# Spreading twelve small loads and re-dealing table work in the first feed-forward block of a decoder trunk

## The chip, the core and the metric

The kernel runs on one core of one Trainium2 chip. The core has five engines that run side by side and wait for one another through semaphores: TensorE (PE, with its weight loads shown apart as PEld), VectorE (DVE), ScalarE (ACT), GpSimd (POOL) and SyncE (SP), which here only issues transfers. Sixteen DMA engines move the data. Every engine takes its instructions in the order in which the program gives them. The metric is the device time of one execution in microseconds, lower is better. The kernel before took 982.28 us (median of three runs, 981.8 to 982.3).

## What is computed

The reference is a two-layer trunk on 256 rows of 1024 columns. Each layer is half a SwiGLU block, a mixer, and half a SwiGLU block; the mixer of layer 0 is a diagonal state-space layer (S5), that of layer 1 is block-sparse attention.

```python
def swiglu(h, w_gate, w_up, w_down):
    return (jax.nn.silu(h @ w_gate) * (h @ w_up)) @ w_down
...
for layer in range(DEPTH):
    h = h + MACARON_WEIGHT * swiglu(rms_norm(h, ffn_norm[layer, 0]), ffn_w_gate[layer, 0],
                                    ffn_w_up[layer, 0], ffn_w_down[layer, 0])
    hn = rms_norm(h, mix_norm[layer])
    ...
    h = h + MACARON_WEIGHT * swiglu(rms_norm(h, ffn_norm[layer, 1]), ffn_w_gate[layer, 1],
                                    ffn_w_up[layer, 1], ffn_w_down[layer, 1])
```

The S5 mixer uses, for each of 64 groups, a state of 64 complex numbers with decay `lam`, an input matrix from `b_re`, `b_im` (64 x 64 x 16 each) and an output matrix from `c_re`, `c_im` (64 x 16 x 64 each):

```python
bu_re = jnp.einsum('bcgn,gpn->bcgp', u_c, bb_re)
...
pr, pi, sr, si = lax.associative_scan(combine, (lam_re_b, lam_im_b, bu_re, bu_im), axis=1)
...
y = jnp.einsum('bcgp,gnp->bcgn', st_re, c_re) - jnp.einsum('bcgp,gnp->bcgn', st_im, c_im)
```

## The kernel before

**Stages.** The phases run one after the other: `f00` (first SwiGLU block), `s5`, `f01`, `f10`, `moba`, `f11`. What this text is about lies in `f00`, where the kernel also works out, beside the matmuls, the tables that `s5` will read.

**Weights.** Each weight is used as a sum of two parts, `whi` and `wlo`, and each product is three matmuls. `Stream` brings the weights as units of 1 MB into three buffers called `raw`, on SP's queue. A unit is then split in two halves, and a split (L86, L87) is an ACT instruction that writes `whi` and a DVE instruction that writes `wlo`. When the second half of a unit is split, its `raw` buffer is free, and the load of the unit three further on is given to SP's queue at that place of the program. SP therefore waits for DVE's `wlo` before each weight load, and everything given to SP later stands behind it. In `f00` a split is only placed once its unit's load lies AGE = 8 slots back.

**Slots.** While `f00` is written out, a counter called slot stands for the progress of TensorE: `fill` adds 0.7 for every three matmuls of 512 columns (1.4 in the first group). Everything that is placed between the matmuls is placed by this counter.

**Groups.** `f00` goes through 11 groups `j` of 256 hidden columns. `gu(j, t)` makes gate and up for half `t` of the rows (8 steps of three matmuls). `gated` then applies SiLU on ACT (L480, `sg`) and multiplies on DVE (L484, `act`). Later `tr(j, t)` transposes `act` on TensorE (L497), and ACT and DVE copy the result as `ah` and `al` (L499, L500). `dn(j, f)` multiplies it with the down weights. I write g(j,a) for the two gate/up units of group j, and d(j) for its down unit. Between `gated(j, t)` and `tr(j, t)` lie 7 slots from group 1 on: `gated(2, 0)` is placed at slot 30.8 and `tr(2, 0)` at 37.8, for instance.

**Tables.** `tables` is a generator which `fill` resumes once per step. It holds three lists. `loads` are twelve transfers, given to SP's queue when the slot reaches the number in LOADS: eight for B (`ld_b4`, 64 KB each, in runs of 16 floats) and four for C (`ld_c2`, 128 KB each, in runs of 64 floats). `work` is DVE's table work in order: the doubling steps of the powers (`e_init`, `e_step`, from slot E_AT = 26), the products of B (`b_all`), then for each of 8 blocks two `muls` and two `sums`, and `spread`. Each item has a price; a credit grows by DENSE times the slots passed, is capped at 1.5, and an item is placed when the credit covers its price. `later` holds pieces that use TensorE: four transposes of C (`c_tr`, L826, from slot C_AT = 44), and for each block a `t3_tab` (L884) and two `t1_tab` (L866), the first LAG = 12 slots after the block's `spread` and at least PACE = 4 slots apart. `spread(b)` may only be placed after three pieces of block b-2 are done, so from the third block on the pieces' pace of 12 slots per block leads. At its end `tables` gives SP the first loads of the finished tables (`TA`, `TE`, `TB`, L951 to L959).

Of the kernel before, what the change touches and what calls it, by code (L numbers as in the profile page):

```python
# [29 lines left out]
AO = (68, 68, 68, 68)  # L30
OO = 68

LOADS = (16, 16.5, 17, 17.5, 18, 18.5, 19, 19.5, 22, 24, 26, 28)
C_AT, E_AT, B_AT, DENSE, LAG, PACE, AGE = 44, 26, 36, 0.46, 12, 4.0, 8.0


class Stream:
# [83 lines left out]
def trunk_kernel(ctx: ExitStack, tc, x, ffn_norm, ffn_w_gate, ffn_w_up, ffn_w_down, mix_norm,  # L121
# [498 lines left out]
    def tables(tp):  # L620
# [26 lines left out]
        def ld_b4(i, c):  # L647
            b = (s5_b_re, s5_b_im)[i]
            nc.sync.dma_start(bn[i][:, 8 * c:8 * c + 8], bass.AP(tensor=b.tensor, offset=b.offset + 16384 * c,
                                                                 ap=[[16, 128], [2048, 8], [1, 16]]))  # L650

        def ld_c2(i, a):
            c = (s5_c_re, s5_c_im)[i]
            nc.sync.dma_start(cn[:, i, 4 * a:4 * a + 4], bass.AP(tensor=c.tensor, offset=c.offset + 32768 * a,
                                                                 ap=[[64, 128], [8192, 4], [1, 64]]))

        loads = [lambda i=i, c=c: ld_b4(i, c) for c in range(4) for i in range(2)]
        loads += [lambda i=i, a=a: ld_c2(i, a) for a in range(2) for i in range(2)]
        yield
        dtb = tp.tile([32, 2, 64], F32, name="dtb")  # L660
        nc.scalar.activation(dtb, ldt[:, :, None].to_broadcast([32, 2, 64]), AF.Exp)
# [258 lines left out]
        done = [-4]  # L920
        dma = list(zip(LOADS, loads))
        credit, then = 0.0, slot[0]
        while work or later or dma:
            now = slot[0]
            credit, then = min(credit + DENSE * (now - then), 1.5), now
            while dma and dma[0][0] <= now:
                dma.pop(0)[1]()
            if later and later[0][0] <= now:
                f = later.pop(0)
                f[1](*f[2:])  # L930
                done[0] += 1
            while work and work[0][1] <= now and credit >= work[0][0] and done[0] >= work[0][4]:
                w, _, f, pe, _ = work.pop(0)
                f[0](*f[1:])
                credit -= w
                t = max([now + LAG] + [a[0] + PACE for a in later])
                later += [(t + PACE * k,) + a for k, a in enumerate(pe)]
            yield
# [386 lines left out]


    tab = tables(tabp) if "s5" in phases else iter(())
    next(tab, None)
    slot = [0]
# [145 lines left out]
```

## Time and profile before

| | |
|---|---|
| median of three runs | 982.28 us |
| the profiled execution's own time | 982.36 us |
| its span on the core | 980.4 us |
| instructions | 17231 |
| time outside the span | 1.96 us |
| `f00`, from its second group to its last transposition | about 21 to 205 us |
| first matmul of `s5` that reads a table (L1009) | 222.5 us |

The page of the profile counts an engine as busy while an instruction of it runs, and names for idle time what ended it. The timeline lists an engine's instructions by start; a row with x2 is two instructions in a row, and a bracket at its end gives the idle time ahead and what ended it. Matmul records overlap (0.39 us long, started every 0.23 us), so a wait shorter than the overlap hides in them; the distance from start to start shows it. SPq rows are the moments at which SP issues a transfer.

### The profile page before, as it was taken

What the parts mean: (1) busy time and instruction counts of PE and PEld (TensorE: products, weight loads), DVE (VectorE), ACT (ScalarE), POOL (GpSimd) and SP (SyncE); (2) the same over time, 40 slices, a digit from 0 to 9 for tenths busy, and PEclk for the clock granted to TensorE, in tenths of its full rate; (3) what the DMA queues carried; (4) which work ended last, traced back from release to release, by engine and by line L of the source; (5) the groups of instructions that cost most, each with busy time, mean ns of one, the idle gap of its engine ahead of it and who ended that gap; (6) DMA issues with size and microseconds to landing.
All of it is one profiled execution on the core that took longest, in us unless ns stands there. A gap on an engine that the chain in (4) does not pass through costs nothing.

```text
span 980.4 us, 17231 instructions
## 1 busy us (share of the span) xinstructions
PE 972.2 (99%) x6727; PEld 867.5 (88%) x6727; DVE 688.8 (70%) x1118; ACT 560.4 (57%) x1008; POOL 186.5 (19%) x364
## 2 busy tenths in 40 slices
PE   9999999999999999999999999999999999999998
PEld 7878888788888999999999999998788899999997
DVE  5799767768768676666667766665789667766662
ACT  7565766553267555555456655544897556655540
POOL 6963544416511000000010000000441010000000
PEclk9999999999999999999999999999999999999999
DMA  8988877887645666565536656562544546656531
GB/s 284 249 269 279 275 261 242 298 324 245 252 173 182 213 208 215 172 212 175 172 125 214 221 173 214 173 215 92 172 145 157 186 143 214 231 174 213 172 130 44
DMA packets 140002, 198.74 MB, mean 203 GB/s; under 512 B 18232, under 2 KB 111504, under 8 KB 139664
## 3 DMA queue, kind: packets, MB, share of 16 engines
q1 hardware_dynamic: 133808, 184.32, 57.5%
q0 software_dynamic: 5536, 12.71, 3.6%
q8 instruction: 53, 0.87, 0.4%
q10 hardware_dynamic: 576, 0.61, 0.3%
q14 instruction: 29, 0.24, 0.1%
HBM read 183.89 MB, written 13.66 MB: 202 GB/s over the span
## 4 chain that ended last, share of the span: by engine, by line
PE 94%; DVE 2%; ACT 2%; issue 1%; POOL 1%; DMA 1%; SPq 0%; POOLq 0%; DVEq 0%; ACTq 0%
PE pM L554 13%; PE pM L553 13%; PE pM L555 13%; PE pA L399 9%; PE pA L401 9%; PE pA L400 9%; PE pM L399 6%; PE pM L400 6%; PE pM L401 6%; PE pA L473 1%; PE pR L1052 1%; PE pR L333 1%; DVE wlo L87 1%; PE pA L1090 1%; PE pR L866 1%
## 5 line engine op out<-in xcount | busy, mean ns | idle before, releaser
L553 PE MATMUL pM<-xa,whi 128*128 128x256 f32 x1056 | 295.7, 280 | 0.0
L554 PE MATMUL pM<-xa,whi 128*128 128x256 f32 x1056 | 294.9, 279 | 0.0
L555 PE MATMUL pM<-xa,wlo 128*128 128x256 f32 x1056 | 294.7, 279 | 0.0
L93 DVE SCALAR_TENSOR_TENSOR wlo<-raw,gT,whi 128x512 fp32r<-128x512 f32 x328 | 228.1, 748 | 71.2 <-ACT whi L92 71.0
L87 DVE TENSOR_TENSOR wlo<-raw,whi 128x1024 fp32r<-128x1024 f32 (+1 forms) x155 | 187.5, 1225 | 56.0 <-ACT whi L86 54.8
L92 ACT ACTIVATE whi<-raw,gT 128x512 fp32r<-128x512 f32 x328 | 213.7, 711 | 16.4 <-PE pA L401 14.6
L554 PEld LDWEIGHTS pM<-xa,whi 128*128 128x128 f32 x1056 | 198.5, 188 | 2.6
L553 PEld LDWEIGHTS pM<-xa,whi 128*128 128x128 f32 x1056 | 198.5, 188 | 2.3
L555 PEld LDWEIGHTS pM<-xa,wlo 128*128 128x128 f32 x1056 | 198.5, 188 | 0.0
L86 ACT ACTIVATE whi<-raw 128x1024 fp32r<-128x1024 f32 (+1 forms) x155 | 158.7, 1049 | 26.1 <-DMA raw<-in_ffn_w_up_dram 9.8
L399 PE MATMUL pA<-whi,ah 128*128 128x512 f32 x352 | 138.8, 394 | 0.0
L400 PE MATMUL pA<-wlo,ah 128*128 128x512 f32 x352 | 137.6, 391 | 0.0
L401 PE MATMUL pA<-whi,al 128*128 128x512 f32 x352 | 137.6, 391 | 0.0
L568 ACT ACTIVATE sg<-gr 128x256 f32<-128x256 f32 x66 | 27.6, 418 | 165.7 <-DVE gr L565 165.7
L399 PE MATMUL pM<-whi,xa 128*128 128x512 f32 (+1 forms) x304 | 122.2, 402 | 0.0
L400 PE MATMUL pM<-wlo,xa 128*128 128x512 f32 (+1 forms) x304 | 115.8, 381 | 0.1
L401 PE MATMUL pM<-whi,xa 128*128 128x512 f32 (+1 forms) x304 | 115.5, 380 | 0.0
L348 POOL TENSOR_TENSOR ms<-ss 128x1 f32<-128x1 f32 x10 | 1.9, 193 | 470.3 <-ACT sq L345 470.3
L401 PEld LDWEIGHTS pA<-whi,al 128*128 128x128 f32 x352 | 66.1, 188 | 14.3
L399 PEld LDWEIGHTS pA<-whi,ah 128*128 128x128 f32 x352 | 66.1, 188 | 11.6
L400 PEld LDWEIGHTS pA<-wlo,ah 128*128 128x128 f32 x352 | 66.2, 188 | 11.3
L565 DVE TENSOR_TENSOR gr<-pM,rrow 128x512 f32<-128x512 f32 x66 | 45.5, 689 | 40.9 <-PE pM L555 40.8
(269 smaller groups left out, 1214.5 us busy)
## 6 DMA issues: line engine op xcount, KB each, us to landing
raw<-in_ffn_w_down_dram SPq DMA_DIRECT2D x44, 1024.0 KB, 5.4
raw<-in_ffn_w_gate_dram SPq DMA_DIRECT2D x80, 512.0 KB, 4.0
raw<-in_ffn_w_up_dram SPq DMA_DIRECT2D x80, 512.0 KB, 5.1
raw<-in_moba_w_qkv_dram SPq DMA_DIRECT2D x12, 1024.0 KB, 5.1
TB<-dB SPq DMA_DIRECT2D x8, 768.0 KB, 6.6
raw<-in_ffn_w_gate_dram SPq DMA_DIRECT2D x16, 256.0 KB, 4.4
raw<-in_ffn_w_up_dram SPq DMA_DIRECT2D x16, 256.0 KB, 4.7
dB<-tt POOLq DMA_DIRECT2D x16, 256.0 KB, 5.1
```

Of the source, the lines that this page charges most:

```text
L86: nc.scalar.activation(hi[:, c], r[:, c], AF.Copy)
L87: nc.vector.tensor_tensor(lo[:, c], r[:, c], hi[:, c].bitcast(F32), op=OP.subtract)
L92: nc.scalar.activation(hi[:, c], r[:, c], AF.Identity, scale=g)
L93: nc.vector.scalar_tensor_tensor(lo[:, c], r[:, c], g, hi[:, c].bitcast(F32), op0=OP.mult, op1=OP.subtract)
L399: mm(o, xh, wh, start=start, stop=False)
L400: mm(o, xh, wl, start=False, stop=False)
L401: mm(o, xl, wh, start=False, stop=stop)
L553: mm(o, a, xh, start=k == 0 and i == 0, stop=False, skip_group_check=True)
L554: mm(o, a, xl, start=False, stop=False, skip_group_check=True)
L555: mm(o, b, xh, start=False, stop=k == 7, skip_group_check=True)
L565: V.tensor_tensor(gr, ps.rearrange("p (i c) -> p i c", i=2), Rr["row"][:, None, :].to_broadcast([128, 2, 256]), op=OP.mult)
L568: nc.scalar.activation(sg, gr[:, 0, :], AF.Silu)
```

## The change

Three things change: the twelve loads get other slots, C's four come ahead of B's eight, and DENSE becomes two numbers with a slot at which the second takes over. Every instruction of the old program is in the new one; only the order on the queues differs.

```diff
-LOADS = (16, 16.5, 17, 17.5, 18, 18.5, 19, 19.5, 22, 24, 26, 28)
-C_AT, E_AT, B_AT, DENSE, LAG, PACE, AGE = 44, 26, 36, 0.46, 12, 4.0, 8.0
+LOADS = (20, 21, 22, 23, 24, 26, 28, 30, 32, 34, 36, 38)
+C_AT, E_AT, B_AT, DENSE, LAG, PACE, AGE = 44, 26, 36, (64, 0.39, 0.51), 12, 4.0, 8.0
...
-        loads = [lambda i=i, c=c: ld_b4(i, c) for c in range(4) for i in range(2)]
-        loads += [lambda i=i, a=a: ld_c2(i, a) for a in range(2) for i in range(2)]
+        loads = [lambda i=i, a=a: ld_c2(i, a) for a in range(2) for i in range(2)]
+        loads += [lambda i=i, c=c: ld_b4(i, c) for c in range(4) for i in range(2)]
...
-            credit, then = min(credit + DENSE * (now - then), 1.5), now
+            credit, then = min(credit + DENSE[1 + (now > DENSE[0])] * (now - then), 1.5), now
```

## The prediction

> **What bounds the kernel now.** I read the page first: TensorE is busy throughout and carries the chain of waits, so a change elsewhere pays only where TensorE stands still.
>
> ```profile
> span 980.4 us, 17231 instructions
> PE 972.2 (99%) x6727; PEld 867.5 (88%) x6727; DVE 688.8 (70%) x1118; ACT 560.4 (57%) x1008; POOL 186.5 (19%) x364
> PE 94%; DVE 2%; ACT 2%; issue 1%; POOL 1%; DMA 1%; SPq 0%; POOLq 0%; DVEq 0%; ACTq 0%
> ```
>
> Next came the sums by stretch over the first block, which show where TensorE (first figure) falls short of a stretch: 0.70 us between 40 and 50, 0.19 between 50 and 60, and only 0.92 in all of 21 to 207 us. In brackets are counts; the last two figures are the DMA share and GB/s.
>
> ```profile
> 20.00:30.00 10.00, 9.97 (x47) 7.65 (x46) 7.29 (x13) 7.45 (x12) 8.55 (x19) 1.00 0.89 303
> 30.00:40.00 10.00, 10.00 (x47) 8.22 (x46) 8.15 (x12) 6.07 (x8) 9.35 (x16) 1.00 0.94 167
> 40.00:50.00 10.00, 9.30 (x44) 7.36 (x43) 7.58 (x21) 3.73 (x6) 9.21 (x25) 1.00 1.07 332
> 50.00:60.00 10.00, 9.81 (x51) 7.91 (x50) 9.96 (x16) 7.34 (x12) 9.92 (x20) 1.00 0.88 259
> ...
> 21.00:207.00 186.00, 185.08 (x980) 149.05 (x980) 145.47 (x219) 115.66 (x185) 97.52 (x169) 1.00 0.85 269
> ```
>
> TensorE's timeline names the two places. Matmuls start every 0.23 us (48.38 to 48.61); the transposition of act(2,0) starts 1.09 us after the matmul ahead of it. So 1.09 - 0.23 = **0.86 us** are lost there. The second, 0.19 us, stands before a transposition of C.
>
> ```profile
> 48.38 0.39 PE L400 MATMUL pM<-wlo,xa 128*128 128x512 f32 x1
> 48.61 0.39 PE L401 MATMUL pM<-whi,xa 128*128 128x512 f32 x1
> 49.70 0.44 PE L497 MATMUL pR<-cst,act 128*128 128x128 f32 x2 [0.70 <-DVE act L484]
> ...
> 59.66 0.63 PE L826 MATMUL pR<-cst,cn 128*64 128x128 f32 x4 [0.19 <-ACT cb L829]
> ```
>
> Then I went back from act(2,0). On DVE it ends at 49.17 + 0.47 = 49.64, behind a split that began at 45.29 after 1.71 us of idling for ACT. On ACT that split waited 6.14 us for a weight load, and `sg` for act(2,0) stood behind it.
>
> ```profile
> 43.28 0.30 DVE L628 TENSOR_TENSOR e<-z,z 128x32 f32<-128x32 f32 x2
> 45.29 1.27 DVE L87 TENSOR_TENSOR wlo<-raw,whi 128x1024 fp32r<-128x1024 f32 x1 [1.71 <-ACT whi L86]
> ...
> 49.17 0.47 DVE L484 SCALAR_TENSOR_TENSOR act<-pM,rr,sg 128x256 f32<-128x256 f32 x1
> ```
>
> ```profile
> 44.20 2.01 ACT L86 ACTIVATE whi<-raw 128x1024 fp32r<-128x1024 f32 x2 [6.14 <-DMA raw<-in_ffn_w_up_dram]
> ...
> 46.38 0.47 ACT L480 ACTIVATE sg<-pM,rr 128x256 f32<-128x256 f32 x1
> ```
>
> The late load is g(3,0), issued at 37.75 and 38.90. Its buffer came free with the second of the two splits from 31.31, at 31.31 + 2.44 = 33.75. SP wasn't waiting for it: from 31.10 on its rows follow without a gap, six loads of B, one of which held the queue 3.36 us.
>
> ```profile
> 31.31 2.44 DVE L87 TENSOR_TENSOR wlo<-raw,whi 128x1024 fp32r<-128x1024 f32 x2
> ...
> 36.85 2.39 DVE L87 TENSOR_TENSOR wlo<-raw,whi 128x1024 fp32r<-128x1024 f32 x2
> ```
>
> ```profile
> 30.69 0.37 SPq L182 DMA_DIRECT2D raw<-in_ffn_w_down_dram  x1
> 31.10 0.47 SPq L649 DMA_DIRECT2D bn<-in_s_b_re_dram  x1
> 31.62 0.58 SPq L649 DMA_DIRECT2D bn<-in_s_b_im_dram  x1
> 32.24 3.36 SPq L649 DMA_DIRECT2D bn<-in_s_b_re_dram  x1
> ...
> 37.75 1.10 SPq L176 DMA_DIRECT2D raw<-in_ffn_w_gate_dram  x1
> 38.90 0.51 SPq L176 DMA_DIRECT2D raw<-in_ffn_w_up_dram  x1
> ```
>
> So the chain is: B's burst on SP, g(3,0) 4.0 us late, ACT idle, DVE idle, act(2,0) late, 0.86 us of TensorE.
>
> **The loads.** The change puts no load between d(1), issued at 30.69, and g(3,0): C begins at slot 20.3, and g(3,0) is given to SP at 19.6. So g(3,0) is issued at 33.75, not 37.75. In this stretch a weight load took 3.9 to 8.7 us to land:
>
> ```profile
> DMA to landing us min/median/max: 3.9/5.2/8.7
> ```
>
> Its second half goes out some 0.5 us later, so it lands between 38.1 and 42.9, about 39.5 by the median. DVE is ready for its split at 43.28 + 0.30 = 43.58, and ACT's part takes 2.01/2 = 1.0 us: even the late end (43.9) costs DVE 0.3 us only. The pieces ahead of act(2,0) are the same in both programs (`e_init` and three `e_step`, slots 26.6 to 29.4). From the split's start to act's end is 49.64 - 45.29 = 4.35 us, so act(2,0) ends at 43.58 + 4.35 = 47.9, at worst 48.2. TensorE comes for it at 48.61 + 0.23 = 48.84. The wait is gone: **-0.86 us**, with 0.6 to 0.9 us to spare. What is late next is act(2,1):
>
> ```profile
> 58.15 0.47 DVE L484 SCALAR_TENSOR_TENSOR act<-pM,rr,sg 128x256 f32<-128x256 f32 x1
> ```
>
> It ended 58.62 - 49.64 = 8.98 us after act(2,0), with a DVE full from 50 to 60, and has the same pieces ahead of it in both programs. It will end at 47.9 + 9.0 = 56.9; its transposition, which stood two instructions ahead of the 59.66 row, is due about 58.2. No wait. The 0.19 at 59.66 is ACT's lateness with C's copies, of the same origin; I take it as gone: **-0.2 us** (bounds 0 and -0.3).
>
> The loads themselves cost what they did. From 20 to 30 us a busy share of 0.89 moved 3.03 MB. From 30 to 40 a share of 0.94 moved 1.67 MB, of which B is 0.5: the 1.17 MB of weights take 8.9 x 1.17/3.03 = 3.4 us, which leaves 6.0 us for B's eight loads, 0.75 us each. They now go out singly or by two or three from slot 24 to 38, each ahead of a weight load by at most 2.3 us, against a burst of 4.5; C's four stand together behind g(3,0), where SP must wait for g(3,1)'s buffer in any case (the first split from 36.85, so 36.85 + 2.39/2 = 38.0). `more_loads`, due at slot 30, comes among B's, long before its first use at slot 50. The needs are far off: C at slot 44, B at 53.2, the last load at 38.5. I cost the rest of the loads at nothing; the cover is that a split is placed 8 slots (8.8 us at the 1.1 worked out below) after its load, against 5.2 to land. If a B load in front uses up that cover, the same kind of wait comes back: +0.9 at most for one.
>
> [...]
>
> **The table work.** The replay of the credit rule gives the slots. With 0.39, DVE's pieces fall behind: the first `spread` comes at 70.7, not 65.8. From there the pace of the TensorE pieces (12 slots a block) leads in both programs, so 0.51 buys little: all `t3_tab` and `t1_tab` come 4.9 slots later and the generator ends at 175.7, not 170.8, still before the last transposition at 176.4. DVE's bunch of a block (one `muls`, two `sums`) stands nearest ahead of an act at 0.7 slots in both: before at 88.9 for the act at 89.6, after at 105.7 for the one at 106.4. The tightest act of before beyond 60 us is the one behind that bunch:
>
> ```profile
> 111.27 0.47 DVE L484 SCALAR_TENSOR_TENSOR act<-pM,rr,sg 128x256 f32<-128x256 f32 x1
> ```
>
> ```profile
> 113.86 0.38 PE L497 MATMUL pR<-cst,act 128*128 128x128 f32 x2
> ```
>
> ```profile
> 85.15 1.22 DVE L628 TENSOR_TENSOR z<-cb,l 128x1024 f32<-128x1024 f32 x1
> 86.40 0.69 DVE L628 TENSOR_TENSOR zc<-z,z 128x512 f32<-128x512 f32 x1
> ```
>
> It was ready 113.86 - 111.74 = 2.1 us early. Before act(4,1) stands one `muls` more than before (1.22 us), within that. I take 0; bounds 0 and +0.5 (a whole bunch, 1.22 + 2 x 0.69 = 2.6 us, against 2.1).
>
> POOL's stores (`dB`, `dA`, `dE`) move with the pieces in unchanged order, on an engine busy 97.52 of 186 us; nothing waits for them before the loads of `s5`, which the end of the tables moves. From tr(2,0) (slot 37.8, due 48.84) to tr(5,1) (slot 96.6, 113.86) a slot takes 65.0/58.8 = 1.1 us, so 4.9 slots are 5.4 us:
>
> ```profile
> 200.18 0.35 SPq L951 DMA_DIRECT2D TA<-dA  x1
> ```
>
> ```profile
> DMA to landing us min/median/max: 3.3/4.3/6.8
> ```
>
> TA goes out at 205.6 at the latest and lands by 212.4, against a first use at 222.5 (222.5 - 1.1 after the gain). That first use:
>
> ```profile
> L1009 PE MATMUL pA<-U,TA x128: 222/222/269, 222.5 to 232.9; 128*64 128x63 f32 x128
> ```
>
> So 9 us cover it; beyond them each us would cost one. The fourth load of `s5_w_in` now goes to SP ahead of TA, the loads for `glu` behind it. Cost 0.
>
> **The sum.** 982.36 is the profiled execution's own time, 1.96 more than its span. 982.36 - 0.86 - 0.2 = 981.3. The median of the runs is 0.08 lower, within their spread of 0.5.
>
> **The rivals.** (1) The wait only moves: DMA work is unchanged, the share is 0.88 to 1.07 until 60 us, and a weight load behind two or three loads of B (2.3 us) makes a later act late by about as much. For it: DVE is full from 50 on. Against it: act(2,1) has 1.3 us to spare by the sum above. It gives back 0.9: 982.2. (2) Slower, DVE as the bound: the pieces moved by 4.9 slots fall ahead of acts that have least to spare. It decides from 2.1 us of added lateness; a whole bunch (2.6) then costs 0.5 us per act, and with one such act in each of groups 4 to 10, 3.5 us: 981.3 + 3.5 = 984.8. For it: DVE's share in the stage is 145.47 of 186. Against it: the equal nearest distance, and the pace that leads in both. (3) Faster than by the waits shown: something in the matmuls' own rhythm. Above 0.92 us there is no idle time in the stage, so nothing in the rows offers it; a gain of 2.5 us (979.8) would need waits of `s5` to go too, which hang on TensorE's own order.
>
> **How the numbers follow.** Chances: forecast 0.72 (981.3, own range 980.8 to 981.8), rival 1 0.16 (982.2), rival 2 0.08 (982.7 to 986, half of it under 984.2), rival 3 0.04 (979.8). About 0.2% (1.96 us) is what a measurement can tell from no change, so faster means under 980.3 (0.04), slower over 984.2 (0.04), the rest is 0.92. The range 980.7 to 982.7 holds the first two cases.
>
> **What would show it.** Right: g(3,0)'s two issues follow d(1)'s within 4 us; ACT's wait of 6.14 us shrinks under 2; L497 near 49 us has no bracket; `f00` ends 1 us sooner. Wrong: a bracket on another L497 or L826 (rival 1), several after 90 us with DVE named (rival 2), or a bracket on L1009 (TA late).

## The result, and the profile after

The changed kernel takes 984.53 us (median of nine runs, 984.01 to 986.23) against 982.29 (nine runs of the kernel before, 981.8 to 983.03). The ratio is 1.0026, with an interval of 1.0016 to 1.0037: slower by a quarter of a per cent, where 981.3 was forecast and 980.7 to 982.7 given as the range. Six of the nine runs lie between 984.0 and 984.5, three between 986.0 and 986.2; the last section says what the granted clock shows of such steps. The profiled execution took 984.21 us.

The page of the changed kernel: the chain that ends last now holds less of TensorE (90% instead of 94%). The three instructions more than before are, on balance, waits for semaphores.

```profile
span 982.1 us, 17234 instructions
PE 90%; DVE 3%; POOL 3%; ACT 2%; DMA 1%; issue 1%; DVEq 0%; POOLq 0%; ACTq 0%
```

What TensorE waited for from 22 to 320 us, first before and then after (total, times, longest). Left out are two waits of `s5` that are the same in both. The other two went, and two new ones came.

```profile
PE pR L497 <- DVE act L484: 0.7, 1, 0.7
...
PE pR L826 <- ACT cb L829: 0.2, 1, 0.2
```

```profile
PE pA L1009 <- DVE U L1000: 2.3, 1, 2.3
...
PE pR L826 <- DVE al L500: 0.8, 1, 0.8
```

**What went.** The timelines of SP, ACT, DVE and TensorE after, around the old stall at 48. g(3,0) is issued 3.1 us behind d(1), with C behind it; ACT waits 1.66 us for it instead of 6.14; act(2,0) ends at 46.76 + 0.47 = 47.23, and its transposition follows the matmul ahead of it by 48.51 - 48.28 = 0.23, the usual distance.

```profile
30.37 0.37 SPq L182 DMA_DIRECT2D raw<-in_ffn_w_down_dram  x1
33.46 0.37 SPq L176 DMA_DIRECT2D raw<-in_ffn_w_gate_dram  x1
...
34.43 0.50 SPq L654 DMA_DIRECT2D cn<-in_s_c_re_dram  x1
```

```profile
39.39 2.01 ACT L86 ACTIVATE whi<-raw 128x1024 fp32r<-128x1024 f32 x2 [1.66 <-DMA raw<-in_ffn_w_up_dram]
```

```profile
46.76 0.47 DVE L484 SCALAR_TENSOR_TENSOR act<-pM,rr,sg 128x256 f32<-128x256 f32 x1
```

```profile
48.28 0.39 PE L401 MATMUL pM<-whi,xa 128*128 128x512 f32 x1
48.51 0.38 PE L497 MATMUL pR<-cst,act 128*128 128x128 f32 x2
```

**What came at 61.** TensorE and DVE after. The fourth C transposition, `c_tr(1, 1)`, starts 61.53 - 60.34 = 1.19 us after the matmul ahead of it, 0.96 more than usual. It waits for `al` of tr(2,1), which ends on a full DVE at 61.06 + 0.41 = 61.47.

```profile
58.06 0.60 PE L826 MATMUL pR<-cst,cn 128*64 128x128 f32 x4
...
60.34 0.39 PE L401 MATMUL pA<-whi,al 128*128 128x512 f32 x1
61.53 0.63 PE L826 MATMUL pR<-cst,cn 128*64 128x128 f32 x4 [0.81 <-DVE al L500]
```

```profile
61.06 0.41 DVE L500 TENSOR_TENSOR al<-pR,ah 128x256 fp32r<-128x256 f32 x1
```

Nothing in the arithmetic joins the two. Before, the same transposition ran 2 us ahead of the same `al`:

```profile
62.18 0.60 PE L826 MATMUL pR<-cst,cn 128*64 128x128 f32 x4
```

```profile
64.16 0.41 DVE L500 TENSOR_TENSOR al<-pR,ah 128x256 fp32r<-128x256 f32 x1
```

What joins them is the buffer. All small transpositions write `pR`, for which two banks of PSUM are kept (the memory in which `pM`, `pA` and `pR` of the rows above lie), and the build decides which of the two each one gets. By the waits that the built instructions carry, in the kernel before `c_tr(1, 1)` was given the bank of `c_tr(1, 0)`, which ACT empties; in the changed one it is given the bank of tr(2,1), which DVE empties with `al`.

**What came in `s5`.** This chain begins at the last store of a table and ends on TensorE. On POOL, before and after, that store is 202.62 - 197.50 = 5.1 us later:

```profile
197.50 0.54 POOL L869 DMA_DIRECT2D dA<-t  x1 [3.28 <-ACT t L868]
```

```profile
202.62 0.57 POOL L869 DMA_DIRECT2D dA<-t  x1 [3.55 <-ACT t L868]
```

On SP, before and after, the loads of two `glu` units (one row for both) and, ahead of them, the first TA, which goes out 207.71 - 200.18 = 7.5 us later:

```profile
207.20 12.54 SPq L182 DMA_DIRECT2D raw<-in_s_w_glu_dram  x2
```

```profile
207.71 0.35 SPq L951 DMA_DIRECT2D TA<-dA  x1
...
213.76 5.43 SPq L182 DMA_DIRECT2D raw<-in_s_w_glu_dram  x2
```

The sums by stretch say what this did to the DMA engines (last two figures: share and GB/s). Before, from 205 to 210, and then two stretches of after:

```profile
205.00:210.00 5.00, 4.90 (x25) 3.81 (x24) 2.42 (x4) 1.59 (x4) 0.00 (x0) 1.00 1.03 390
```

```profile
205.00:210.00 5.00, 4.86 (x24) 3.76 (x23) 3.12 (x6) 1.25 (x4) 0.00 (x0) 1.00 0.32 125
...
225.00:230.00 5.00, 5.00 (x56) 4.46 (x55) 2.03 (x4) 0.52 (x2) 3.01 (x3) 1.00 1.02 406
```

From 205 to 210, where SP held TA back for the store until 207.71, they were busy for a third of the time (0.32); in the last of these stretches they are full (1.02). The second `glu` load went out at 218.81, no later than before (219.4), but needed 11.1 us to land behind all of that, where it had needed 5.5. Before, its split found the weights there, and the copy of U behind it waited for TensorE alone (ACT, then TensorE):

```profile
226.01 1.05 ACT L86 ACTIVATE whi<-raw 128x1024 fp32r<-128x1024 f32 x1
229.03 0.47 ACT L999 ACTIVATE us<-pM,rr 128x256 f32<-128x256 f32 x1 [1.97 <-PE pM L401]
```

```profile
231.00 2.08 PE L1009 MATMUL pA<-U,TA 128*64 128x63 f32 x64
```

From the chain of waits, then ACT, DVE and TensorE, after:

```profile
218.81 11.10 DMA raw<-in_s_w_glu_dram
```

```profile
229.93 1.06 ACT L86 ACTIVATE whi<-raw 128x1024 fp32r<-128x1024 f32 x1 [4.49 <-DMA raw<-in_s_w_glu_dram]
230.90 0.46 ACT L999 ACTIVATE us<-pM,rr 128x256 f32<-128x256 f32 x1
```

```profile
231.02 1.22 DVE L87 TENSOR_TENSOR wlo<-raw,whi 128x1024 fp32r<-128x1024 f32 x1 [3.85 <-ACT whi L86]
232.16 0.44 DVE L1000 STREAM_TRANSPOSE U<-us 128x256 f32<-128x256 f32 x1
```

```profile
229.96 0.39 PE L401 MATMUL pM<-whi,xa 128*128 128x512 f32 x1
232.66 2.03 PE L1009 MATMUL pA<-U,TA 128*64 128x63 f32 x62 [2.30 <-DVE U L1000]
```

The split of these weights, which nothing needs yet, stands on ACT and on DVE ahead of the copies of U (the projected rows that `s5` works on; L999, L1000), which TensorE does need. TensorE loses 232.66 - 229.96 - 0.23 = 2.5 us, where it lost 0.1 before.

**The account.** The row 48.61 of before stands at 48.28 after: 0.33 us came earlier already in the start-up. That is scatter between executions: experiment 9 runs the same order up to there, and d(1), which SP issues at 30.37 in the changed kernel and at 30.69 before, goes out at 30.79 in it. By its weight load, the first norm transposition behind `f00` (L333) comes at 207.48 instead of 208.05, 0.57 earlier. Of this, 0.33 is the start-up and 0.09 the balance of the waits in `f00` (0.86 + 0.19 - 0.96); the other 0.15 is not traced. From there to the first weight load of `f01` (L553, 310.74 and 312.48) it takes 2.31 us more. 982.36 - 0.57 + 2.31 is 984.1, and the time outside the span is 0.1 us longer.

### The profile page after: what moved, and what is told of

The parts are those of the page before. It is cut to its first block, busy times and chain, and to the rows that moved or that the text cites. A ratio compares the mean times of both kernels' runs of the same rounds, so it can differ in the third digit from the quotient of the medians.

```text
span 982.1 us, 17234 instructions
## 1 busy us (share of the span) xinstructions
PE 971.7 (99%) x6727; PEld 867.5 (88%) x6727; DVE 688.6 (70%) x1118; ACT 560.6 (57%) x1008; POOL 183.6 (19%) x364
## 4 chain that ended last, share of the span: by engine, by line
PE 90%; DVE 3%; POOL 3%; ACT 2%; DMA 1%; issue 1%; DVEq 0%; POOLq 0%; ACTq 0%
PE pM L554 13%; PE pM L553 13%; PE pM L555 13%; PE pA L399 9%; PE pA L401 9%; PE pA L400 9%; PE pM L399 5%; PE pM L400 5%; PE pM L401 5%; DVE wlo L87 1%; DMA raw<-in_s_w_glu_dram 1%; PE pR L1052 1%; POOL sc L682 1%; PE pR L333 1%; PE pA L1090 1%
## 5 line engine op out<-in xcount | busy, mean ns | idle before, releaser
L553 PE MATMUL pM<-xa,whi 128*128 128x256 f32 x1056 | 295.7, 280 | 0.0
L553 PEld LDWEIGHTS pM<-xa,whi 128*128 128x128 f32 x1056 | 198.5, 188 | 2.3
```

What stands on the lines that cost most here:

```text
L553: mm(o, a, xh, start=k == 0 and i == 0, stop=False, skip_group_check=True)
```

## Experiments

Theory Q, as the expectations call it, is that the 2.3 us before L1009 come from the tables' later end by the way just shown; theory B, from experiment 7 on, is that the wait at 61 comes from the PSUM bank. Each run was compared with runs of the kernel before on the same chip; their medians were 982.68 us in the first four experiments, 983.02 in the next four and 982.85 in the last three, so ratios are the better measure.

**1. The loads alone** (from the changed kernel).

```diff
-DENSE = (64, 0.39, 0.51)
+DENSE = (64, 0.46, 0.46)
```

> The loads' part of the change alone: C first and the new slots, table work dealt at 0.46 throughout, so the tables end at slot 170.8 as before. Theory Q (the later end of the tables is what costs: SP stands at the first TA load, the glu loads behind it land late, ACT's split holds up the copies of U): no wait before the first matmul of the second table block (L1009), TA issued near 199.5, and the 0.86 us near 48 us still won: 981.3. Rival R (the new places of the loads cost, through the DMA engines or the fourth load of s5_w_in now ahead of TA): the wait of about 2.4 us at L1009 stays: 983.5 or more. On the wait of 0.96 us before a transposition of C near 61 us: gone if the thinner dealing makes it, there if the later B loads make it (+1.0).

983.69 us, ratio 1.0016 (1.0007 to 1.0024). The wait before L1009 is absent and so is the stall at 48, but the wait at 61 is larger than in the changed kernel. TensorE and DVE of this run:

```profile
63.22 1.06 PE L826 MATMUL pR<-cst,cn 128*64 128x128 f32 x4 [2.20 <-DVE al L500]
```

```profile
62.75 0.41 DVE L500 TENSOR_TENSOR al<-pR,ah 128x256 fp32r<-128x256 f32 x1
```

So the loads' part of the change brings the wait at 61, and the thinner dealing makes it smaller (0.8), since `al` of tr(2,1) then ends earlier (at 61.47 instead of 63.16). This alone makes the loads a loss.

**2. The dealing alone** (from the kernel before).

```diff
-DENSE = 0.46
+DENSE = (64, 0.39, 0.51)
-credit + DENSE * (now - then)
+credit + DENSE[1 + (now > DENSE[0])] * (now - then)
```

> The dealing's part alone: 0.39 to slot 64 and 0.51 after it, the loads as before the change; the tables end at slot 175.7. Theory Q: the wait at L1009 appears, 2.4 us, TA issued near 206 to 208; the 0.86 us near 48 us stay lost: 982.3 + 2.4 = 984.7, and 985.7 if the thinner dealing also makes the wait before the transposition of C. Rival R: no wait at L1009: 982.3.

984.91 us, ratio 1.0026 (1.0016 to 1.0037). TensorE's waits in this run: the one before L1009 is there, the stall at 48 stays, and L826 waits for ACT and not for DVE, so the bank is that of before.

```profile
PE pA L1009 <- DVE U L1000: 1.9, 1, 1.9
...
PE pR L497 <- DVE act L484: 1.0, 1, 1.0
PE pR L826 <- ACT cb L829: 0.4, 1, 0.4
```

**3. The changed kernel with an earlier end of the tables.**

```diff
-LAG = 12
+LAG = 7.1
```

> The whole change with LAG 7.1 for 12: the first table piece on TensorE comes at slot 78.4 and the tables end at 170.8, as before the change; everything up to slot 77 is as in the change. Theory Q: no wait at L1009: 984.5 - 2.4 = 982.1 (the wait near 61 us stays). Rival R: as the change, 984.5.

985.09 us, ratio 1.0027 (1.0015 to 1.0038): no gain. The wait before L1009 is gone, as Q says, but TensorE has two new ones, for an earlier U copy and for a table piece that is now placed too early:

```profile
PE pM L399 <- ACT us L999: 1.9, 1, 1.9
PE pR L866 <- ACT kt L888: 1.6, 1, 1.6
```

The first of these has the same pattern with another unit in it: SP gives out the last unit of `s5_w_in` at 210.28, behind TA at 204.65, and its split, for which ACT waits 2.96 us, stands ahead of U.

The edit moved more than it was meant to, so it decides little.

**4. The kernel before with a later end of the tables** (5.6 slots by the credit rule), nothing else.

```diff
-LAG = 12
+LAG = 16
```

> The kernel before with LAG 16 for 12: only the table pieces on TensorE come later, the tables end at slot 176.4 (the change: 175.7); loads and dealing as before. Theory Q: the wait at L1009 appears, 2.4 to 3 us: 984.7 to 985.3. Rival R: 982.3.

988.48 us, ratio 1.0056 (1.0044 to 1.0069). The profiled execution took 985.68, 3.3 more than the profiled one of before, with TA at 209.74 and 2.1 us of waiting before L1009. ACT stands at the same split:

```profile
230.65 1.06 ACT L86 ACTIVATE whi<-raw 128x1024 fp32r<-128x1024 f32 x1 [4.24 <-DMA raw<-in_s_w_glu_dram]
```

A later end of the tables is enough to make the wait. The median lies higher than this, because four of the six runs took 988.4 to 990.5. Those four have a mean granted clock of 0.995 to 0.998, the other two 1.0 (see the last section); no profile of this kernel shows where.

**5. The split out of U's way** (from the changed kernel; `P` places a split).

```diff
-w256.0:7 P t1 w512.0:0 w256.1:4-7 w512.0:1 r1
+w256.0:7 t1 w512.0:0 w256.1:4-7 P w512.0:1 r1
```

> The changed kernel, with one word of the order in `s5` moved: the split of the second `glu` unit (L86 on ScalarE, L87 on VectorE) is issued behind the two U copies instead of between them. Loads, table work and every time on the DMA queues stay. Theory Q (the 2.3 us wait before L1009 is the U copy that stands on ScalarE behind a split whose weights land 11 us after their issue): that wait goes, the weights still land at about 230, the stall of 0.8 us before the C transposition at 61 stays; time 984.3 less 2.3 = 982.0, between 981.8 and 982.5 in most runs. Rival R (U comes late because projection work or the TA tables themselves are late): the wait before L1009 stays at over 1.5 us, time 984 to 984.6.

982.67 us, ratio 0.9999 (0.9990 to 1.0009); profiled 981.86. The weights land as late as ever, at 229.0, but U is copied ahead of their split and TensorE has no wait there. The 2.3 us are gone with one instruction moved: Q is right, R falls.

```profile
228.43 0.47 ACT L999 ACTIVATE us<-pM,rr 128x256 f32<-128x256 f32 x1 [2.90 <-PE pM L401]
229.05 1.06 ACT L86 ACTIVATE whi<-raw 128x1024 fp32r<-128x1024 f32 x1 [0.15 <-DMA raw<-in_s_w_glu_dram]
```

**6. Less ahead of the weights on the DMA engines** (from the changed kernel).

```diff
-        for b in range(3):
+        for b in range(1):
             ld_b(b)
...
             if b + 3 < NB:
                 ld_a(b + 3)
+            if b < 2:
+                ld_b(b + 1)
```

> The changed kernel, with the second and third TB table (768 KB each) asked for after the first and second L1009 block instead of in one go with TA and TE; nothing else is moved. Theory Q in its full form (the weights land late because 5.6 MB of tables and one `glu` unit, held up until 207.7 by the wait for the last dA store, are still on their way when they are asked for at 218.8): 1.5 MB less stands ahead, some 3.8 us at the 400 GB/s of this stretch, so they land at about 226, the wait before L1009 shrinks from 2.3 us to under 0.5, time 982.0 to 982.8. If the late landing has another cause (these weights' own load is slow): landing stays at 11 us, wait 2.3 us, time 984 to 984.6. If TB is then itself late for the first y block: a new wait at L1052, time 983 or more.

982.49 us, ratio 0.9996 (0.9986 to 1.0005); profiled 982.14. With 1.5 MB of TB behind them the weights are there in time: asked for at 219.1, they have landed when the split runs at 225.65 without a wait, within 6.5 us instead of 11.1, in the order of the changed kernel.

```profile
225.65 1.05 ACT L86 ACTIVATE whi<-raw 128x1024 fp32r<-128x1024 f32 x1
228.65 0.47 ACT L999 ACTIVATE us<-pM,rr 128x256 f32<-128x256 f32 x1 [1.96 <-PE pM L401]
```

So the late landing was the backlog of tables, and both ends of the chain (5 and 6) undo it.

**7. The loads alone with the old bank** (from experiment 1). The two banks get names of their own and are taken in turn; `c_tr(1, 1)` takes no turn.

```diff
-    def psR():
-        return pp.tile([128, 512], F32, name="pR", tag="R", bufs=2)
+    def psR(step=1, n=[0]):
+        n[0] ^= step; return pp.tile([128, 512], F32, name="pR", tag=f"R{n[0]}", bufs=1)
...
         def c_tr(i, a):
-            ps = psR()
+            ps = psR(int((i, a) != (1, 1)))
```

> The loads' new places and order alone (dealing of the table work as before, as in the first run of this study), with the PSUM bank of the small transpositions taken in turn, except that the fourth C transposition takes the bank of the third one, as it did in the kernel before; the order of all instructions stays. Theory B (the wait before the C transposition at 61 comes from the bank: in the changed kernel it was given the bank of tr(2,1), which al(2,1) on the full VectorE frees only at 63.2): the wait of 2.2 us is gone, and with it the half clock behind it; the stall at 48 stays away; time 983.4 - 2.2 = 981.2, between 980.9 and 981.6. Rival D (VectorE is simply too late with its splits because B's loads push the weights' loads back): the wait moves to the next instruction that needs VectorE (the gate's transposition or act(3,0)), over 1.5 us of it stay, time 983 or more.

981.1 us, ratio 0.9981 (0.9972 to 0.9991): 2.6 us under experiment 1. The transposition now runs at 61.33, 2.1 us ahead of the same `al`, and TensorE is busy 185.99 of 186 us from 21 to 207, against 185.08 before.

```profile
61.33 0.60 PE L826 MATMUL pR<-cst,cn 128*64 128x128 f32 x4
```

```profile
63.45 0.41 DVE L500 TENSOR_TENSOR al<-pR,ah 128x256 fp32r<-128x256 f32 x1
```

```profile
21.00:207.00 186.00, 185.99 (x985) 149.98 (x983) 146.61 (x220) 116.17 (x186) 100.72 (x170) 1.00 0.86 271
```

D falls: DVE is as late as it was, and nothing else waits for it.

**8. The kernel before with the new bank.** The same edit, but `c_tr(1, 1)` takes its turn like the others.

> The kernel before, with the PSUM bank of the small transpositions taken strictly in turn, so that its fourth C transposition waits for al(2,1) as in the changed kernel; loads, dealing and order stay. Theory B: al(2,1) ends at 64.57 there and the transposition stood at 62.18, so it waits 2.3 to 2.5 us; the gate's transposition no longer waits 0.1 to 0.4; time 982.5 + 2.2 = 984.7, and some runs 1.7 more where a stretch of half clock follows. Rival D: the bank costs nothing measurable there, 982.3 to 982.8.

985.89 us, ratio 1.0032 (1.0020 to 1.0043). The wait appears in the kernel that never had it, for the same `al`, which here ends at 65.09:

```profile
65.14 1.06 PE L826 MATMUL pR<-cst,cn 128*64 128x128 f32 x4 [2.19 <-DVE al L500]
```

**9. Both repairs in the changed kernel** (the edits of 6 and 7).

> The changed kernel with both repairs: the fourth C transposition takes the third one's bank, and the second and third TB are asked for after the first and second L1009 block. New places of the loads and thinner dealing stay. Theory B and Q: the waits of 0.8 at 61 and of 2.3 before L1009 are gone, none takes their place; time 984.3 - 0.8 - 2.3 = 981.2, between 980.9 and 981.6. If it comes out at the run of the loads alone with that bank (981.1), the thinner dealing by itself is worth nothing; under 980.8 would mean that it gains, over 981.6 that it still costs something elsewhere.

981.24 us, ratio 0.9984 (0.9976 to 0.9993); profiled 981.27. TensorE waits for nothing from 44 to 68 and from 215 to 240 us, and is busy 185.86 of 186 us from 21 to 207.

It beats the kernel before and the changed one. Experiment 7 (ratio 0.9981) deals the table work as before and has no edit on TB; the intervals of the two overlap. So with both waits repaired the thinner dealing brings nothing that these runs can tell.

**10 and 11. Which part of the loads' change clears the stall at 48** (both from experiment 7). Ten has C first in the old slots, eleven the new slots with B first.

```diff
-LOADS = (20, 21, 22, 23, 24, 26, 28, 30, 32, 34, 36, 38)
+LOADS = (16, 16.5, 17, 17.5, 18, 18.5, 19, 19.5, 22, 24, 26, 28)
```

> The loads' order alone: C first, in the old places (16 to 19.5, then 22, 24, 26, 28), dealing as before, fourth C transposition in the third one's bank. Forecast's reason (the stall at 48 goes because the places let g(3,0) be asked for ahead of the loads): here eight loads stand ahead of g(3,0) again, it is asked for at about 37 to 38, and the wait of 0.9 us before tr(2,0) stays; 982.0 to 982.5. Rival (the order is what counts, C's loads being lighter for the queues than B's): wait gone, 981.1 to 981.4.

```diff
-        loads = [lambda i=i, a=a: ld_c2(i, a) for a in range(2) for i in range(2)]
-        loads += [lambda i=i, c=c: ld_b4(i, c) for c in range(4) for i in range(2)]
+        loads = [lambda i=i, c=c: ld_b4(i, c) for c in range(4) for i in range(2)]
+        loads += [lambda i=i, a=a: ld_c2(i, a) for a in range(2) for i in range(2)]
```

> The loads' new places alone, B first as before, dealing as before, fourth C transposition in the third one's bank. Forecast's reason: g(3,0) is asked for at about 33.5, so the stall at 48 goes; C is now asked for last, between 50 and 55, and the C transpositions stand at 54, 56, 58 and 61, so one to three of them wait for their loads, 0.5 to 3 us together; time 981.5 to 984. Rival (the places do all of it and C has time enough): 981.1 to 981.4.

Ten: 983.47 us, ratio 1.0009 (1.0000 to 1.0019), somewhat over the expected 982.0 to 982.5. g(3,0) is issued at 37.63 behind six of the loads, and the stall stays (SP, then TensorE's waits):

```profile
31.02 0.47 SPq L654 DMA_DIRECT2D cn<-in_s_c_re_dram  x1
...
37.63 0.53 SPq L176 DMA_DIRECT2D raw<-in_ffn_w_gate_dram  x1
```

```profile
PE pR L497 <- DVE act L484: 1.0, 1, 1.0
```

Eleven: 983.13 us, ratio 1.0011 (1.0002 to 1.0020). g(3,0) is issued at 33.58, the stall is gone, and the first C transposition waits for its load instead:

```profile
PE pR L826 <- DMA cn<-in_s_c_re_dram: 2.2, 1, 2.2
```

The places free g(3,0); the order is needed because C, last in the new places, comes 2.2 us late.

## Why the prediction was wrong

**The stall at 48 (forecast -0.86): right, in size and way.** g(3,0) went out at 33.46 (forecast 33.75), act(2,0) ended at 47.23 (47.9, of which 0.33 is the earlier start), 1.3 us ahead of TensorE. Experiments 10 and 11 show that the place did it. act(2,1) ended at 56.60 (56.9), without a wait.

**The C transposition at 59.66 (forecast -0.2): right for that one**, which runs at 58.06 without a bracket. With the two, experiment 7 gains 0.91 us of busy time in `f00` against 1.06 forecast, nearly all of the 0.92 that was missing there.

**"I cost the rest of the loads at nothing": wrong, +0.96 us.** The cover that was named, 8 slots between a load and its split, held; what failed was the assumption that the edit moves only instructions. It also turned over which PSUM bank `c_tr(1, 1)` gets, and so made it wait for a DVE instruction: more differs than the order on the queues. The diff and the order of TensorE's instructions do not show that; the waits of each instruction do. By itself (experiments 1 and 8) it costs 2.2 us. How the build picks a bank no run shows; that experiment 2 kept the old one says that it was the loads that turned it.

**The table work in `f00` (forecast 0, up to +0.5): right.** Experiments 7 and 9 differ in it (and in the place of two TB loads), and their ratios are 0.9981 and 0.9984. Rival 2, which priced it, gave nearly the measured time (984.8) by a mechanism that did not occur: luck.

**The tables' end ("Cost 0"): wrong, +2.4 us (2.5 against 0.1), the greater part.** The last store came 5.1 us later, as worked out (5.4). TA did not go out "at 205.6 at the latest" but at 207.71, because that store took 207.71 - 202.62 = 5.1 us to its release of TA instead of 200.18 - 197.50 = 2.7. It took 4.8, 5.9 and 5.4 us in experiments 2, 3 and 4, which also differ from the kernel before in DENSE or LAG. Why stays open. In the two us behind its issue the DMA engines were busier (1.02 after, from 202 to 204, against 0.44 before, from 198 to 200), in part with the fourth load of `s5_w_in`, which now went out ahead of TA; but in experiment 3 that load went out behind TA and the store took 5.9 us all the same. The cover of 9 us was right for TA, which landed before its use. The step that failed is the sentence that the loads for `glu` stand behind TA: it was written down and not followed. The second of them is asked for no later than before; its price is the backlog ahead of it on the DMA engines (11.1 us to land instead of 5.5), and then ACT and DVE, whose order puts its split ahead of U. The prediction would have taken a bracket on L1009 for a late TA; the bracket came, and its releaser, U, says otherwise.

**The rivals.** A wait that only moves (rival 1) is what happened at 61, by another cause than a DMA queue. None of the cases held the `glu` chain, so the range was too narrow at its upper end. With the two unforeseen waits taken out, experiment 9 takes 981.27 us in its profiled execution: the forecast sum. That the two agree so closely is in part luck, since the levels differ between chips (982.29 to 983.02 us for the kernel before): beside the kernel before on the same chip, experiment 9 gains 1.6 us by the medians and experiment 7 1.9, more than the 1.06 forecast, and no profile of the kernel before on those chips shows where the rest lies.

## What to carry to other kernels

When work is moved to a later end, follow every transfer that stands behind it on the queue to the engine that consumes it, and look there for what is queued behind that consumer: here a load whose split weights TensorE first reads at 260.95 (L1092) held up, at 229.93, a copy that was needed at once, and TensorE lost 2.5 us. When transfers or instructions are moved, compare also which buffer each tile gets and what each instruction waits for, since two unrelated tiles in one bank made an ordering here that the code does not contain (a wait of 0.81 us in the changed kernel, 2.20 and 2.19 in experiments 1 and 8). A wait that appears somewhere new is read by its releaser before it is read by its place.

## What the runs showed of the hardware

In the profiles of three kernels a wait of TensorE of 1.9 to 2.2 us was followed by a stretch at half clock. Sums by stretch of experiment 1, whose transposition at 63.22 had waited 2.20 us (the figure ahead of the DMA share is the granted clock):

```profile
58.00:63.00 5.00, 3.02 (x17) 2.22 (x15) 5.00 (x8) 1.81 (x5) 5.00 (x10) 1.00 1.11 344
63.00:66.50 3.50, 3.28 (x10) 2.70 (x11) 2.57 (x6) 0.75 (x2) 3.03 (x7) 0.52 1.09 369
```

In slices of 0.5 us the clock is 0.50 from 63.5 to 66.5, and matmuls that start every 0.23 us elsewhere start every 0.43 there (64.51, 64.94, 65.36, 65.79). A clock of 0.52 over 3.5 us is 3.5 x 0.48/0.5 = 3.4 us at half speed, which by this count cost 3.5 x 0.48 = 1.7 us of matmuls, an estimate. The profiles of experiment 8 (0.83 from 63 to 66 and 0.60 from 66 to 69, behind the wait of 2.19) and of experiment 3 (0.52 from 226 to 228 and 0.75 from 228 to 231, behind its wait of 1.9) show the same: by the same count 3.4 us at half speed each. Not every such wait does it: the profiled run of the changed kernel waited 2.3 us before L1009 and kept its full clock (1.00 in each stretch of 5 us from 225 to 240).

The mean clock of each run gives an estimate of how often: it is 0.997, 0.998 and 0.997 in the profiled runs of experiments 1, 3 and 8. Seven kernels have a wait of 1.9 us or more in their profile (the changed one and experiments 1, 2, 3, 4, 8 and 11): 21 of their 59 runs have a mean clock of 0.998 or less. In experiments 5, 6, 7, 9 and 10, where no wait from 44 to 68 and from 215 to 240 us (for 7, from 44 to 68) is longer than 1.0 us, none of 51 runs has, and of the runs of the kernel before beside the experiments 1 of 76. The three longer runs of experiment 8 (986.8 to 987.0, against 985.0 for the other three) are of this kind, and so are two of the three runs of the changed kernel at 986 (0.997 and 0.998). The third kept its full clock and was no longer on the core than the others (982.0 us); its time lies outside the span.
